# Two sets of sixteen staged tiles, each tile 32 bytes longer, in a two-layer trunk

## The chip, the cores and the metric

The kernel runs on one core of a Trainium2 chip. The metric is the device time of one execution in microseconds.

## What is computed

The reference is a trunk of two layers over 256 tokens of width 2048, in float32. Every sub-layer is preceded by an RMS norm and added to the residual `h`:

```
layer 0   z = gelu(h @ w_in[2048, 4096]); u, v = split(z); v = rms_norm(v)
          s = causal 128x128 mixing of v per head; h += (u * s) @ w_out[2048, 2048]
layer 1   u = h @ w_in[2048, 2048]; y = a diagonal state-space scan of u
          ga, gb = split(gelu(y) @ w_glu[2048, 4096]); h += ga * sigmoid(gb)
after each layer
          z = h @ w_up[2048, 11264]; z = causal convolution of width 3 along the tokens
          gate, val = split(z); h += (silu(gate) * val) @ w_down[5632, 2048]
at the end  rms_norm(h)
```

## The kernel before

**Products in three terms.** TensorE multiplies in the type float32r. To keep float32 accuracy each operand is held as two tiles, a high part and a rest. A weight chunk `w` becomes `wh` (cast on ScalarE, line 124) and `wl` (`w - wh` on VectorE, line 125). The activations, transposed so that the feature dimension is on the partitions, are held the same way: one tile of 128 partitions x 512 columns per chunk of 128 features, with the high parts of the 256 tokens in columns 0 to 255 and the rests in columns 256 to 511.

**X and Gt.** There are two such sets of sixteen tiles. `X[0..15]` holds the normed input of a sub-layer (written by `stage_x`). `Gt[0..15]` holds the input of the product that ends a sub-layer (written by `split_to` or, in the state-space layer, by `emit`). In the second product of layer 1 the same memory as `X` (tag `X0` to `X15`) holds half sums under the name `kept`.

**Two forms of product.** In `group_b_steps` (lines 892 to 894) and in `form_b_steps` (lines 986 to 988) the activation slice is the stationary operand, 128 columns (512 bytes a partition) of an `X` or `Gt` tile, and 512 columns of `wh` or `wl` (2,048 bytes) move past it. For each chunk `k` and each half of the tokens there are three matmuls:

```python
                    T.matmul(ps[:, tt, :], xh, wh, start=k == k_first, stop=False)
                    T.matmul(ps[:, tt, :], xh, wl, start=False, stop=False)
                    T.matmul(ps[:, tt, :], xl, wh, start=False, stop=k == ktot - 1)
```

so six matmuls in a row read one staged tile, and the next six read the next tile. In `form_a_steps` (lines 785 and 786) it is the other way round: 128 columns of `wh` or `wl` are stationary and 512, then 256, columns of an `X` tile move. Every matmul has a weight load of its own, which TensorE begins while the matmul ahead of it is still running.

**Order of the work.** Class `Weights` brings the weights in by DMA on the queue of SyncE (three buffers `raw`), splits them in units of 1024 columns (five buffers each of `wh` and `wl`) and stays four units ahead of the products. The products of the up-projections read `X`, those of the down-projections and of `w_out` and `w_glu` read `Gt`. The FFN goes in three parts of 14, 16 and 14 chunks: an up-projection of two chunk pairs at a time, after it `activate` for each chunk (four transposes into `zt`, the convolution, Silu into a tile `s`, the product with the second half in place, then `split_to(Gt[k], s)`), and then four groups of the down-projection. The scheduler of the tile framework orders each engine's instructions by their dependences.

**Where the tiles lie.** Tiles of the pool `const` are laid out in the order in which they are first asked for, each at a multiple of 32 bytes. After `hn` come `Gt[0..15]` of 2,048 bytes each, then `rbc` (1,024), `rho` (512), `nss` (64), `rtok`, `tv` and `tt_` (8 bytes in 32 each), then `X[0..15]` of 2,048 bytes each, and behind the pool the weight buffers, all of them multiples of 512 bytes long. Modulo 512 every `X` tile therefore begins at the same offset as every weight buffer, and every `Gt` tile at an offset 160 bytes below that (1,024 + 512 + 64 + 96 = 1,696 = 3 x 512 + 160). All slices that a matmul reads lie at multiples of 512 bytes inside their tile or buffer.

Of the kernel before, what the change touches and what calls it, by code (L numbers as in the profile page):

```python
# [9 lines left out]
F32 = mybir.dt.float32  # L10
F32R = mybir.dt.float32r
# [6 lines left out]
P = 128  # L18
D = 2048
NT = 256  # L20
KC = D // P
# [647 lines left out]
def tile_hybrid_trunk(  # L669
# [10 lines left out]
    const = ctx.enter_context(tc.tile_pool(name="const", bufs=1))  # L680
# [54 lines left out]
    conv = const.tile([P, 4, 2 * HC], F32, name="conv")  # L735
    hn = const.tile([P, 2, D], F32, name="hn")
    X = [None] * KC
    Gt = [const.tile([P, 2 * NT], F32R, name=f"Gt{k}") for k in range(KC)]
    rbc = const.tile([P, NT], F32, name="rbc")
    rho = const.tile([P, NH], F32, name="rho")  # L740
    nss = const.tile([P, 2, 8], F32, name="nss")
    rtok = const.tile([P, 2], F32, name="rtok")
    tv = const.tile([P, 2], F32, name="tv")
    tt_ = const.tile([P, 2], F32, name="tt_")

    scr = []
    for name, n in (
# [54 lines left out]

    def stage_x(k, g_col, src):

        xk = X[k] = const.tile([P, 2 * NT], F32R, name=f"X{k}", tag=f"X{k}", bufs=1)
        A.mul(xk[:, :NT], src, g_col[:, k : k + 1])
        V.scalar_tensor_tensor(
            xk[:, NT:], src, g_col[:, k : k + 1], xk[:, :NT].bitcast(F32), ALU.mult, ALU.subtract
        )
# [97 lines left out]
    def ffn(l, g_next, fin=None):  # L907
        cw = conv

        def activate(z, c, q, k):  # L910

            pt = misc_ps.tile([P, 512], F32, name="zt", tag="misc")
            for v in range(2):
                for tt in range(2):
                    T.transpose(  # L915
                        pt[:, v * NT + tt * P : v * NT + (tt + 1) * P],
                        z[:, tt, v * NT + q * P : v * NT + (q + 1) * P], ident,
                    )
            a = fpool.tile([P, 2, NT], F32, name="a", tag="a", bufs=2)
            for v in range(2):  # L920
                cv = c + v * HC
                zt = pt[:, v * NT : (v + 1) * NT]
                A.activation(a[:, v], zt, AF.Identity, bias=cw[:, 3, cv : cv + 1], scale=cw[:, 2, cv : cv + 1])  # L923
                V.scalar_tensor_tensor(  # L924
                    a[:, v, 1:], zt[:, : NT - 1], cw[:, 1, cv : cv + 1], a[:, v, 1:], ALU.mult, ALU.add
                )
                V.scalar_tensor_tensor(  # L927
                    a[:, v, 2:], zt[:, : NT - 2], cw[:, 0, cv : cv + 1], a[:, v, 2:], ALU.mult, ALU.add
                )
            s = fpool.tile([P, NT], F32, name="s", tag="s", bufs=2)  # L930
            A.activation(s, a[:, 0], AF.Silu)
            V.tensor_tensor(s, s, a[:, 1], op=ALU.mult)
            split_to(Gt[k], s)

        for pi, (c0, n, ups, downs) in enumerate(ffn_groups(l)):
            last = pi == len(FFN_PARTS) - 1
            for i in range(n // 2):

                def evac(ps, i=i):
                    z = fpool.tile([P, 2, 512], F32, name="z", tag="z", bufs=2)  # L940
                    for tt in range(2):
                        A.mul(z[:, tt], ps[:, tt], rtok[:, tt : tt + 1])  # L942
                    for q in range(2):
                        pending.append(lambda q=q: activate(z, c0 + 2 * i + q, q, 2 * i + q))

                group_b(X, [4] * 4, evac, {k: (lambda k=k: bg(BG_UP[k])) for k in range(4)})
            nks = [4] * (n // 4) + ([n % 4] if n % 4 else [])
            bgs = {i: (lambda: bg(BG_DOWN)) for i in range(len(nks) - 1)}
            for g in range(4):
                if fin is None or not last:  # L950
                    group_b(Gt, nks, lambda ps, g=g: residual(fpool, g, ps, g_next if last else None), bgs)
                elif g < 3:
                    group_b(Gt, nks, lambda ps, g=g: fin(g, [ps[:, tt, :] for tt in range(2)], (0, 1)))
                else:
                    pss = [acc_ps.tile([P, 2, 512], F32, name="accb", tag="acc")[:, 0, :] for tt in range(2)]
                    form_b(Gt, nks, pss, 10, lambda: fin(g, pss, (0,)))
                    fin(g, pss, (1,))
# [202 lines left out]
    with tc.tile_pool(name="s5", bufs=1) as sp:  # L1160

        Ys = [None] * KC

        def emit(s, yt):
            g, yv = Gt[s], yt.rearrange("p (j k) -> p k j", j=4)
            hi, lo = (g[:, i * NT : (i + 1) * NT].rearrange("p (k j) -> p k j", j=4) for i in range(2))
            A.copy(hi, yv)
            V.tensor_tensor(lo, yv, hi.bitcast(F32), op=ALU.subtract)
            Ys[s] = g

        s5 = S5Tokens(tc, sp, misc_ps, scr, rho, emit)
        rbv = rbc.rearrange("p (k j) -> p j k", j=4)
        sched = {}

        def at(slot, fn, *a):
            sched.setdefault(slot, []).append((fn, a))

        for s in range(KC):
            n = N_OF[s]
            at(n - 1, s5.load, s)  # L1180
            at(n - 1, s5.load1, s)
            at(n, s5.drive, s)
            at(n + 1, s5.take, s)
            at(n + 1, s5.scan, s)
            at(n + 1, s5.load2, s)
            at(n + 2, s5.turn, s)
            at(n + 3, s5.outputs, s)
            at(n + 4, s5.gelu, s)
            at(n + LAT[0], s5.fetch, s)
            at(n + LAT[1], s5.finish, s)  # L1190
        order = (
            s5.gelu, s5.take, s5.finish, s5.fetch, s5.turn, s5.scan, s5.outputs, s5.drive, s5.load2, s5.load, s5.load1
        )

        n_slot = [0]

        def step():
            for fn, a in sorted(sched.pop(n_slot[0], []), key=lambda e: order.index(e[0])):
                fn(*a)
            n_slot[0] += 1  # L1200

        for gi in range(8):

            def evac(p, ps, gi=gi):
                t = sp.tile([P, 2, NT], F32, name="t", tag="t", bufs=tmp[0][1])
                A.copy(t, ps[:, :, NT:])
                z = sp.tile([P, 2, NT], F32, name="z", tag="z", bufs=2)
                V.tensor_tensor(z, ps[:, :, :NT], t, op=ALU.add)
                for i in range(2):
                    s = 2 * gi + i  # L1210
                    u = s5.new_u(s)
                    V.tensor_tensor(u, z[:, i].rearrange("p (k j) -> p j k", j=4), rbv, op=ALU.mult)
                    s5.send(s)

            after = {i: step for i in range(2)}
            if gi == 0:
                after[0] = lambda: (drain(2), make_rbc(sp), step())
            form_a(X, [8, 8], [0, 128], evac, after)

        kept = {}  # L1220

        def glu_keep(i):


            def evac(ps):
                kept[i] = [const.tile([P, 512], F32, name=f"kept{i + a}", tag=f"X{i + a}", bufs=1) for a in range(2)]
                for a in range(2):
                    A.copy(kept[i][a], ps[:, a, :])

            return evac  # L1230

        def glu_evac(i):
            def evac(ps):
                for a in range(2):
                    z = sp.tile([P, 512], F32, name="z", tag="z", bufs=2)
                    V.tensor_tensor(z, ps[:, a, :], kept[i][a], op=ALU.add)
                    A.activation(z[:, NT:], z[:, NT:], AF.Sigmoid)
                    V.tensor_tensor(z[:, :NT], z[:, :NT], z[:, NT:], op=ALU.mult)
                    hv = hn[:, a, i * P : (i + 2) * P]
                    V.tensor_tensor(hv, hv, z[:, :NT], op=ALU.add)  # L1240
                    square_sum(sp, hv, nss[:, a, i // 2 : i // 2 + 1])
                pending.append(lambda: stage_pair(i // 2, cols[:, 3]))
                if i == KC - 2:
                    total_r(nss, 8, rtok)

            return evac

        fa = group_b_steps(Ys, [4, 4], glu_keep(0))
        fb = group_b_steps(Ys, [4, 4], glu_keep(2))
        for f in (fa, fb, fa, fb):  # L1250
            next(f)
            step()
        for f in (fa, fb):
            for _ in f:
                pass
        for i in range(4, KC, 2):
            group_b(Ys, [4, 4], glu_keep(i), {0: step, 1: step})
        assert not sched
        craw = fetch_conv(sp, 1)
        for i in range(0, KC, 2):  # L1260
            group_b(Ys, [4, 4], glu_evac(i), {1: (lambda: place_conv(craw))} if i == 0 else None, 8)
# [69 lines left out]
```

## Time and profile before

| | |
|---|---|
| time, median of 3 runs | 2145.45 us (2145.39 to 2145.92) |
| the profiled execution: its own time | 2145.46 us |
| the profiled execution: span from first to last instruction | 2143.8 us |
| TensorE (PE) busy | 2115.5 us, 99% of the span |
| mean granted TensorE clock | 0.994 |
| VectorE (DVE), ScalarE (ACT), GpSimd (POOL) busy | 1439.3, 1134.9, 90.5 us |
| DMA | 438.59 MB, mean 205 GB/s |

The span is 1.7 us shorter than the time of the execution that it belongs to. Matmuls are pipelined: the end of one is modelled, so the durations of neighbours overlap, and what a matmul costs a chain of matmuls is the step from its start to the start of the next.

### The profile page before, as it was taken

The page shows a single profiled execution, that of the slowest core. Times are in us where ns is not written, and L with a number is a line of the kernel's source. Part 1 is how long each engine was busy: PE and PEld are TensorE (multiplying, and loading weights), DVE is VectorE, ACT ScalarE, POOL GpSimd, SP SyncE. Part 2 cuts the span into 40 slices and gives each one's busy share as a digit, 9 for nine tenths or more (in the row PEclk, how much of TensorE's full clock was granted, in tenths as well). Part 3 has the DMA queues.
Part 4 walks back from the last instruction along what each step waited for, and adds up shares of the span by engine and source line. Part 5 has one row for each costly group of instructions (what it writes and reads, how often), then busy time and mean ns, then how long its engine had stood idle before and what let it go on. Part 6 is the DMA issues. An engine that isn't in the chain of part 4 may idle for free.

```text
span 2143.8 us, 27328 instructions
## 1 busy us (share of the span) xinstructions
PE 2115.5 (99%) x10279; PEld 1740.3 (81%) x10279; DVE 1439.3 (67%) x2123; ACT 1134.9 (53%) x1656; POOL 90.5 (4%) x142
## 2 busy tenths in 40 slices
PE   9999999999999999999998999999999999999998
PEld 7888888888888778888887788888888888888886
DVE  5476677886896645888678766766655656546564
ACT  6544456554555534555456655555544555345553
POOL 1010000000111110000000000000000000000000
PEclk9999999999999999999999999999999999999999
DMA  8655556666777666565799986565556555555553
GB/s 277 199 180 183 188 177 199 222 218 229 215 240 232 217 207 192 189 218 198 231 254 262 271 260 196 177 207 186 176 183 198 189 186 187 181 193 181 192 177 118
DMA packets 358597, 438.59 MB, mean 205 GB/s; under 512 B 31712, under 2 KB 275520, under 8 KB 357824
## 3 DMA queue, kind: packets, MB, share of 16 engines
q1 hardware_dynamic: 349008, 407.94, 60.2%
q0 software_dynamic: 9424, 28.88, 4.6%
q8 instruction: 81, 1.33, 0.3%
q14 instruction: 52, 0.43, 0.1%
q10 hardware_dynamic: 32, 0.01, 0.0%
HBM read 414.66 MB, written 22.02 MB: 204 GB/s over the span
## 4 chain that ended last, share of the span: by engine, by line
PE 95%; DMA 3%; DVE 1%; ACT 1%; issue 0%; SPq 0%; ACTq 0%; DVEq 0%; POOLq 0%
PE accb L892 26%; PE accb L893 26%; PE accb L894 26%; PE acc L785 4%; PE acc L786 2%; PE zt L915 2%; PE accv L986 1%; PE accv L987 1%; PE accv L988 1%; DMA tab<-rd 1%; PE pt L820 1%; PE ps_x L584 1%; DMA w<-in_b_w_glu_dram 0%; DMA ud<-u 0%; ACT wh L124 0%
## 5 line engine op out<-in xcount | busy, mean ns | idle before, releaser
L125 DVE TENSOR_TENSOR wl<-w,wh 128x1024 fp32r<-128x1024 f32 (+1 forms) x721 | 879.3, 1222 | 601.9 <-ACT wh L124 597.8
L124 ACT CAST wh<-w 128x1024 fp32r<-128x1024 f32 (+1 forms) x721 | 754.4, 1050 | 769.4 <-PE accb L894 636.8
L894 PE MATMUL accb<-wh,X 128*128 128x512 f32 x1408 | 552.3, 392 | 0.0
L892 PE MATMUL accb<-wh,X 128*128 128x512 f32 x1408 | 551.7, 392 | 0.0
L893 PE MATMUL accb<-wl,X 128*128 128x512 f32 x1408 | 549.2, 390 | 0.0
L892 PE MATMUL accb<-wh,Gt 128*128 128x512 f32 x1060 | 423.2, 399 | 0.0
L894 PE MATMUL accb<-wh,Gt 128*128 128x512 f32 x1060 | 421.7, 398 | 0.0
L893 PE MATMUL accb<-wl,Gt 128*128 128x512 f32 x1060 | 421.6, 398 | 0.0
L894 PEld LDWEIGHTS accb<-wh,X 128*128 128x128 f32 x1408 | 264.3, 188 | 56.8
L893 PEld LDWEIGHTS accb<-wl,X 128*128 128x128 f32 x1408 | 264.4, 188 | 54.6
L892 PEld LDWEIGHTS accb<-wh,X 128*128 128x128 f32 x1408 | 264.4, 188 | 54.0
L894 PEld LDWEIGHTS accb<-wh,Gt 128*128 128x128 f32 x1060 | 200.3, 189 | 48.4 <-issue 0.2
L892 PEld LDWEIGHTS accb<-wh,Gt 128*128 128x128 f32 x1060 | 200.1, 189 | 48.1
L893 PEld LDWEIGHTS accb<-wl,Gt 128*128 128x128 f32 x1060 | 200.3, 189 | 47.8 <-issue 0.2
L785 PE MATMUL acc<-X,wh 128*128 128x512 f32 x512 | 185.2, 403 | 0.0
L786 PE MATMUL acc<-X,wl 128*128 128x256 f32 x512 | 145.2, 284 | 0.0
L785 PEld LDWEIGHTS acc<-X,wh 128*128 128x128 f32 x512 | 97.7, 191 | 22.0
L923 ACT ACTIVATE a<-zt,conv 128x256 f32<-128x256 f32 x176 | 94.5, 558 | 14.5 <-PE zt L915 8.2
L786 PEld LDWEIGHTS acc<-X,wl 128*128 128x128 f32 x512 | 98.3, 192 | 0.2
L942 ACT ACTIVATE z<-accb,rtok 128x512 f32<-128x512 f32 x88 | 55.8, 685 | 65.8 <-PE accb L894 65.7
L924 DVE SCALAR_TENSOR_TENSOR a<-zt,conv,a 128x255 f32<-128x255 f32 x176 | 77.6, 476 | 13.3 <-ACT a L923 13.3
L927 DVE SCALAR_TENSOR_TENSOR a<-zt,conv,a 128x254 f32<-128x254 f32 x176 | 77.1, 474 | 0.7
(299 smaller groups left out, 1407.1 us busy)
## 6 DMA issues: line engine op xcount, KB each, us to landing
w<-in_f_w_up_dram SPq DMA_DIRECT2D x352, 512.0 KB, 4.6
w<-in_f_w_down_dram SPq DMA_DIRECT2D x80, 1024.0 KB, 5.2
w<-in_b_w_glu_dram SPq DMA_DIRECT2D x64, 512.0 KB, 5.2
w<-in_a_w_in_dram SPq DMA_DIRECT2D x28, 1024.0 KB, 5.3
w<-in_a_w_out_dram SPq DMA_DIRECT2D x16, 1024.0 KB, 5.1
w<-in_b_w_in_dram SPq DMA_DIRECT2D x16, 1024.0 KB, 8.5
w<-in_f_w_down_dram SPq DMA_DIRECT2D x16, 512.0 KB, 3.7
tab<-rd SPq DMA_DIRECT2D x32, 256.0 KB, 6.9
```

What stands on the lines that cost most here:

```text
L124: self.nc.scalar.copy(hi[:, a:b], raw[:, o + a : o + b])
L125: self.nc.vector.tensor_tensor(lo[:, a:b], raw[:, o + a : o + b], hi[:, a:b].bitcast(F32), op=ALU.subtract)
L785: T.matmul(ps, wh, Xt[k], start=k == k_first, stop=False, skip_group_check=True)
L786: T.matmul(ps[:, NT:], wl, Xt[k][:, :NT], start=False, stop=k == ktot - 1, skip_group_check=True)
L892: T.matmul(ps[:, tt, :], xh, wh, start=k == k_first, stop=False)
L893: T.matmul(ps[:, tt, :], xh, wl, start=False, stop=False)
L894: T.matmul(ps[:, tt, :], xl, wh, start=False, stop=k == ktot - 1)
L915: T.transpose(pt[:, v * NT + tt * P : v * NT + (tt + 1) * P], z[:, tt, v * NT + q * P : v * NT + (q + 1) * P], ident,)
L923: A.activation(a[:, v], zt, AF.Identity, bias=cw[:, 3, cv : cv + 1], scale=cw[:, 2, cv : cv + 1])
L924: V.scalar_tensor_tensor(a[:, v, 1:], zt[:, : NT - 1], cw[:, 1, cv : cv + 1], a[:, v, 1:], ALU.mult, ALU.add)
L927: V.scalar_tensor_tensor(a[:, v, 2:], zt[:, : NT - 2], cw[:, 0, cv : cv + 1], a[:, v, 2:], ALU.mult, ALU.add)
L942: A.mul(z[:, tt], ps[:, tt], rtok[:, tt : tt + 1])
```

## The change

Every tile of `Gt` and of `X` (and of `kept`, which uses the memory of `X`) gets eight more float32 columns, 32 bytes, that nothing reads or writes; the name stays bound to the first 512 columns. So tile `k` begins 32·`k` bytes further on, modulo 512, than tile 0. A tile `pad` of 224 bytes is added behind `tt_`. The sixteen `Gt` tiles then take 512 bytes more, `X[0]` and the weight buffers stay at one common offset modulo 512, `Gt[0]` stands 384 bytes below that offset (160 + 224) or, the same thing modulo 512, 128 above it. Relative to the weight buffers `X[k]` begins at 32·`k` and `Gt[k]` at 128 + 32·`k`, modulo 512. The sizes add up to 1,248 bytes a partition, and `s` of the FFN goes from two buffers to one (1,024 bytes less in that pool).

```diff
-    Gt = [const.tile([P, 2 * NT], F32R, name=f"Gt{k}") for k in range(KC)]
+    Gt = [const.tile([P, 2 * NT + 8], F32R, name=f"Gt{k}")[:, : 2 * NT] for k in range(KC)]
...
     tt_ = const.tile([P, 2], F32, name="tt_")
+    const.tile([P, 56], F32, name="pad")
...
-        xk = X[k] = const.tile([P, 2 * NT], F32R, name=f"X{k}", tag=f"X{k}", bufs=1)
+        xk = X[k] = const.tile([P, 2 * NT + 8], F32R, name=f"X{k}", tag=f"X{k}", bufs=1)[:, : 2 * NT]
...
-            s = fpool.tile([P, NT], F32, name="s", tag="s", bufs=2)
+            s = fpool.tile([P, NT], F32, name="s", tag="s", bufs=1)
...
-                kept[i] = [const.tile([P, 512], F32, name=f"kept{i + a}", tag=f"X{i + a}", bufs=1) for a in range(2)]
+                kept[i] = [const.tile([P, 520], F32, name=f"kept{i + a}", tag=f"X{i + a}", bufs=1)[:, :512] for a in range(2)]
```

## Rows read from the trace of the kernel before

**Rows 1.** The page: the span, the engines' busy time and instructions.

```profile
span 2143.8 us, 27328 instructions
PE 2115.5 (99%) x10279; PEld 1740.3 (81%) x10279; DVE 1439.3 (67%) x2123; ACT 1134.9 (53%) x1656; POOL 90.5 (4%) x142
```

**Rows 2.** The chain of work that ended last, shares of the span by engine.

```profile
PE 95%; DMA 3%; DVE 1%; ACT 1%; issue 0%; SPq 0%; ACTq 0%; DVEq 0%; POOLq 0%
```

**Rows 3.** Costliest groups: line, operation, shapes, count; busy us, mean ns; idle before.

```profile
L894 PE MATMUL accb<-wh,X 128*128 128x512 f32 x1408 | 552.3, 392 | 0.0
...
L892 PE MATMUL accb<-wh,Gt 128*128 128x512 f32 x1060 | 423.2, 399 | 0.0
...
L785 PE MATMUL acc<-X,wh 128*128 128x512 f32 x512 | 185.2, 403 | 0.0
...
L986 PE MATMUL accv<-wh,X 128*128 128x512 f32 x128 | 51.0, 398 | 0.0
...
L986 PE MATMUL accb<-wh,Gt 128*128 128x512 f32 x28 | 10.9, 396 | 0.0
```

**Rows 4.** Timeline of PE, an up-projection: start us, duration us (55 matmuls in all).

```profile
1699.71 0.39 PE L893 MATMUL accb<-wl,X 128*128 128x512 f32 x1
1699.94 0.39 PE L894 MATMUL accb<-wh,X 128*128 128x512 f32 x1
1700.16 0.39 PE L892 MATMUL accb<-wh,X 128*128 128x512 f32 x1
...
1711.95 0.39 PE L893 MATMUL accb<-wl,X 128*128 128x512 f32 x1
```

**Rows 5.** Timeline of PE, a down-projection (31 matmuls in all).

```profile
744.88 0.39 PE L892 MATMUL accb<-wh,Gt 128*128 128x512 f32 x1
745.12 0.39 PE L893 MATMUL accb<-wl,Gt 128*128 128x512 f32 x1
...
751.91 0.40 PE L893 MATMUL accb<-wl,Gt 128*128 128x512 f32 x1
```

**Rows 6.** Timeline of PE, an up-projection after transposes: nine steps, then four.

```profile
345.50 0.39 PE L892 MATMUL accb<-wh,X 128*128 128x512 f32 x1
...
347.59 0.39 PE L892 MATMUL accb<-wh,X 128*128 128x512 f32 x1
...
348.49 0.39 PE L893 MATMUL accb<-wl,X 128*128 128x512 f32 x1
```

**Rows 7.** Timeline of PE, products of the first form: five pairs, then three pairs.

```profile
159.25 0.39 PE L785 MATMUL acc<-X,wh 128*128 128x512 f32 x1
...
160.98 0.39 PE L785 MATMUL acc<-X,wh 128*128 128x512 f32 x1
...
170.41 0.39 PE L785 MATMUL acc<-X,wh 128*128 128x512 f32 x1
...
171.47 0.40 PE L785 MATMUL acc<-X,wh 128*128 128x512 f32 x1
```

**Rows 8.** Stretches of 4 and 5: busy us (count) by engine, PEclk, DMA share, GB/s.

```profile
1700.00:1712.00 12.00, 12.00 (x55) 9.94 (x54) 9.61 (x17) 6.65 (x11) 0.00 (x0) 1.00 0.57 185
744.00:752.00 8.00, 8.00 (x44) 6.41 (x35) 4.13 (x5) 3.57 (x7) 2.08 (x2) 1.00 0.68 197
```

**Rows 9.** Timelines of ACT and DVE around two Silus.

```profile
566.40 0.41 ACT L931 ACTIVATE s<-a 128x256 f32<-128x256 f32 x1
...
567.15 0.41 ACT L931 ACTIVATE s<-a 128x256 f32<-128x256 f32 x1
...
571.80 0.43 DVE L801 TENSOR_TENSOR Gt<-s,Gt 128x256 fp32r<-128x256 f32 x1
```

**Rows 10.** Who waited for whom: us in total, times, longest us.

```profile
ACT wh L124 <- PE accb L894: 636.8, 453, 3.7
...
PE ps_x L584 <- DVE wl L125: 2.8, 1, 2.8
```

**Rows 11.** The stretch of the state-space layer, columns as in Rows 8.

```profile
1080.00:1260.00 180.00, 165.85 (x1116) 138.74 (x1115) 144.89 (x186) 111.50 (x164) 8.42 (x15) 0.95 1.01 269
```

## The prediction

> **What bounds the kernel now.** I read the engines' busy time first: TensorE is busy for 2115.5 of 2143.8 us [rows 1], and the chain of work that ended last is 95% TensorE [rows 2]. So nothing but the pace of its matmuls is worth much, and an edit that touches only SBUF addresses can act through that pace alone. The costliest groups give the counts: three lines of 1408 and three of 128 with an `X` tile as stationary operand, 4608 matmuls in all; three of 1060 and three of 28 with a `Gt` tile, 3264; and 512 pairs of the first form, in which `X` moves [rows 3]. The first two kinds are the same instruction, 128x128 against 512 columns, and yet the mean modelled duration is 392 ns with `X` and 399 with `Gt` [rows 3]. The ends are modelled, so I went to the timeline for the steps from start to start. In a clean stretch of an up-projection 54 steps take 12.24 us, 226.7 ns each [rows 4]; in a down-projection 30 steps take 7.03 us, 234.3 ns each [rows 5]. [...] The other engines don't explain the 7.6 ns: in the faster stretch VectorE is busy for 80% and ScalarE for 55% (9.61 and 6.65 of 12 us), in the slower one for 52% and 45% (4.13 and 3.57 of 8 us) [rows 8]. What differs by the layout is where the stationary tile begins against the weight buffer: at the same offset modulo 512 for `X`, 160 bytes below it for `Gt`.
>
> A third reading decides my forecast. Just after transposes the matmuls on `X` don't run at 226.7 ns: nine steps take 2.09 us, and only then do four take 0.90 us [rows 6]. Four steps at 226.7 would be 0.907, so the start between the two runs is shown some 0.007 us late; the nine then take 2.083 us, 231.5 ns each. The fast pace of `X` is thus one into which the chain of matmuls settles, over some nine steps in which address and form stay alike. The first form has two paces as well: five pairs in 1.73 us, 346 ns, and three pairs in 1.06 us, 353 ns [rows 7].
>
> **The change part by part.** *The staggered tiles.* After the change the stationary tile stands at sixteen offsets against the weight buffer, and the offset changes after every six matmuls, when the product goes on to the next tile. The chain had to stay alike for nine steps to settle; now it stays alike for six. I therefore take the unsettled pace, 231.5 ns, for both kinds.
> - `X`: 231.5 - 226.7 = 4.8 ns x 4608 = 22.1 us. Part of it is paid already: `activate` runs once for each of the 88 FFN chunks, and if half of these interrupt products on `X`, 44 x 9 x 4.8 ns = 1.9 us. Left: +20.2 us.
> - `Gt`: 231.5 - 234.3 = -2.8 ns x 3264 = -9.1 us.
> - First form: moving tile and stationary weights part in the same way; 0 to 512 x 7 ns = 3.6 us, and since both paces occur now I take +2 us.
>
> No row shows a residue other than the two, so both ends stay open. From below, the shortest step that the rows show, rounding included, is 0.22 us (the second to the third matmul on `X`, as 0.23 and 0.22 alternate to give 226.7) [rows 4]: at 220 ns everywhere, -6.7 x 4608 - 14.3 x 3264 = -77.6 us. From above, 0.24 us [rows 5]: 13.3 x 4608 + 5.7 x 3264 = +79.9 us. My value lies between the two settled paces and is the only one that a chain of changing state shows.
>
> [...]
>
> *The common shift of `X[0]` and the weight buffers* (1,248 bytes in all at the buffers) moves both operands of the `X` products alike. I cost it at nothing: matmuls on half-tiles and on second buffer halves, multiples of 512 bytes apart, mix in the stretch of 54 even steps [rows 4]. DMA writes the same bytes to other offsets; in the product stretches the DMA share is 0.57 and 0.68 [rows 8], so landings have cover. Only the state-space stretch has none: DMA 1.01 there, TensorE busy for 165.85 of 180 us [rows 11]. If a fifth of its 14 us went or came, that is 3 us either way; I take 0.
>
> *VectorE, ScalarE on the moved tiles*: same instructions, and ScalarE alone waits 636.8 us for TensorE to free weight buffers [rows 10]. Nothing.
>
> *One buffer `s`.* Before, two Silus run 0.75 us apart and the first `s` is read last at 571.80 + 0.43 = 572.23 us [rows 9]. With one buffer the second Silu comes up to 572.23 - 567.15 = 5.1 us later. If it stood in ScalarE's queue in place, the next casts of weights would stand behind it, then the subtraction on VectorE, then TensorE. What hides it: the split runs four units ahead, and a unit is 12 matmuls, 12 x 0.23 = 2.7 us, so 11 us; TensorE waits for `wl` once in the whole execution, for 2.8 us [rows 10]. The tile `Gt[k]` it feeds is wanted a group later. I take 0; with the cover gone in one place, 5 us.
>
> Sum: 20.2 - 9.1 + 2 = +13.1 us on the profiled execution's own 2145.46 us, which is the median of the runs, 2145.45, within 0.01: **2158.6 us**.
>
> **The rivals.**
> *Slower, as summed* (0.50). For it: the settling [rows 6], and that equal offsets are the faster of the two cases that the trace has, so that fifteen of sixteen `X` tiles leave the better case. Against it: two points say little of fourteen others. Its own range: at a step of 230 ns, 3.3 x 4608 - 4.3 x 3264 = +1.2 us and 2147; at the pace of `Gt` everywhere, 7.6 x 4608 = +35 us and 2181.
> *Faster: most offsets are better than both* (0.34). If the stationary and the moving reads disturb each other where they meet, and most of the sixteen offsets keep them apart, `Gt` falls to the pace of `X` and `X` keeps it: -7.6 x 3264 = -24.8 us, 2120.7; if steps reach 0.22 us, 2068. It decides once the mean step over the sixteen offsets is below 229.3 ns, since today's weighted mean is (226.7 x 4608 + 234.3 x 3264) / 7872 = 229.9 and 0.2% of the time is 0.55 ns a step. For it: a difference of 7.6 ns from the offset alone shows that something is to be had. Against it: the case that should be worst by that reasoning, equal offsets, is the better one.
> *No effect* (0.10): the change doesn't do what it says, because the two paces come from something else in the two kinds of product, and the offsets are all alike to the reads. Then 2145. [...] For it: the trace has no third offset. Against it: same form, same clock, and busier neighbours in the faster stretch.
> *The single `s` holds ScalarE* (0.06): the second Silu stands in place where the split is least ahead. The hold of 5.1 us less the longest spare wait of ScalarE, 3.7 us [rows 10], is 1.4 us an occurrence; at a handful of places 5 to 10 us on top of an unchanged pace, 2150 to 2155. It decides when the split's lead is under 5.1 us.
>
> **How the numbers follow.** A measurement of this kernel tells 0.2%, 4.3 us, from no change. Of the first case some 0.04 falls within that; the second is faster throughout; the third is the same; the fourth is slower. Faster 0.34, same 0.14, slower 0.52. The predicted time is that of the first case. The range must hold signs of both kinds: at its low end I leave out the deeper third of the faster case (0.12), at its upper end what lies at and above the pace of `Gt` everywhere (0.07): 2112 to 2182 us. The likeliest case's own range is 2147 to 2181.
>
> **What would show it.** In the timeline of an up-projection the step should no longer be 226.7 ns but change every six matmuls, with a mean near 231.5; in a down-projection it should fall below 234.3. Both mean modelled durations, 392 and 399, should meet near 396. Two Silus should no longer stand 0.75 us apart, and TensorE's waits for `wl` should stay at a few us. The forecast is wrong if the mean steps of both kinds come out below 229 ns (the reads were kept apart), if they stay at 226.7 and 234.3 (offsets don't matter), or if TensorE shows new waits for `wh` or `wl` (the single `s`).

## The result, and the profile after

The changed kernel takes 2160.99 us, the median of 3 runs (2159.54 to 2161.01), against 2145.45 before: a ratio of 1.007, with a 95% interval of 1.0052 to 1.0088. It is slower by 11 to 19 us. The forecast was 2158.6, range 2112 to 2182.

The page of the changed kernel first: span, engines, the chain, and the costliest groups (line, operation, shapes, count; busy us, mean ns; idle before). They answer to [rows 1 to 3]; the line numbers have grown by one.

```profile
span 2159.3 us, 27322 instructions
...
PE 2132.4 (99%) x10279; PEld 1738.9 (81%) x10279; DVE 1440.9 (67%) x2123; ACT 1134.0 (53%) x1656; POOL 90.3 (4%) x142
...
PE 95%; DMA 3%; SPq 0%; DVE 0%; ACT 0%; issue 0%; ACTq 0%; DVEq 0%; POOLq 0%
...
L893 PE MATMUL accb<-wh,X 128*128 128x512 f32 x1408 | 560.4, 398 | 0.0
L895 PE MATMUL accb<-wh,X 128*128 128x512 f32 x1408 | 559.8, 398 | 0.0
L894 PE MATMUL accb<-wl,X 128*128 128x512 f32 x1408 | 555.5, 394 | 0.0
L893 PE MATMUL accb<-wh,Gt 128*128 128x512 f32 x1060 | 421.6, 398 | 0.0
L894 PE MATMUL accb<-wl,Gt 128*128 128x512 f32 x1060 | 419.5, 396 | 0.0
L895 PE MATMUL accb<-wh,Gt 128*128 128x512 f32 x1060 | 419.2, 397 | 0.0
L786 PE MATMUL acc<-X,wh 128*128 128x512 f32 x512 | 183.6, 400 | 0.0
```

The count of TensorE's instructions is the same, its busy time has grown by 16.9 us, and the span by 15.5. The chain still belongs to TensorE. The two kinds of product, 392 and 399 ns in [rows 3], now have nearly one mean. The starts in the timeline give the step: a long stretch of a down-projection (346 steps from the first row to the second), then of the up-projection behind it (118 steps from the third row to the fourth).

```profile
1828.29 0.40 PE L894 MATMUL accb<-wl,Gt 128*128 128x512 f32 x1
...
1908.79 0.39 PE L895 MATMUL accb<-wh,Gt 128*128 128x512 f32 x1
1909.02 0.40 PE L893 MATMUL accb<-wh,X 128*128 128x512 f32 x1
...
1936.45 0.40 PE L894 MATMUL accb<-wl,X 128*128 128x512 f32 x1
```

80.50 us / 346 = 232.7 ns with `Gt`, against 234.3 [rows 5]; 27.43 us / 118 = 232.5 ns with `X`, against 226.7 [rows 4]. One kind lost what the other only partly gained.

**The whole difference, summed.** For an account without remainder I gave each matmul of TensorE the time from its start to the next start in the trace, gaps included, and summed by kind. "Mean step" is the mean of those under 262 ns, that is without the gaps.

| us in the profiled execution | before | after | difference | forecast |
|---|---|---|---|---|
| `X` stationary (4608) | 1059.0, mean step 227.2 ns | 1083.2, 232.5 ns | +24.2 | +20.2 |
| `Gt` stationary (3264) | 772.6, 234.2 ns | 766.2, 232.5 ns | -6.4 | -9.1 |
| first form (1024) | 189.1 | 186.1 | -3.0 | +2 |
| all else on TensorE (transposes, state space, gaps) | 111.8 | 112.5 | +0.7 | 0 |
| sum | | | +15.5 | +13.1 |

Part of what differs from one execution to the next is TensorE's granted clock, which was 0.50 in short stretches: 25.9 us of the profiled execution before (mean granted clock 0.994) and 15.4 us of the one after (0.996). Among 23 other runs of the kernel before, the shortest (2140.03 us) had a mean clock of 0.997 and the longest (2149.01) one of 0.992. Four of the six stretches before stand in the state-space layer, each during or just behind a step of 2.1 to 3.9 us in which TensorE waited. By the mean steps alone, which leave such stretches and the gaps out, `X` and `Gt` would cost 5.3 ns x 4608 - 1.7 ns x 3264 = +18.9 us, where the account has +17.8.

The two parts costed at nothing can be read too. ScalarE's timeline at the two Silus of [rows 9]:

```profile
572.53 0.41 ACT L932 ACTIVATE s<-a 128x256 f32<-128x256 f32 x1
...
578.05 0.42 ACT L932 ACTIVATE s<-a 128x256 f32<-128x256 f32 x1 [0.41 <-DVE Gt L802]
```

They stand 5.5 us apart, no longer 0.75, and the second was released by the split that reads the first `s`. Behind it nothing is late. These are the four largest of TensorE's waits for others (us in total, times, longest us); `wh` and `wl` are not among them, nor further down the list:

```profile
PE ps_x L584 <- DMA ubd<-ud: 9.8, 4, 5.8
PE pt L821 <- DMA hn<-in_x_dram: 2.4, 1, 2.4
PE ps_x L584 <- DVE sp L625: 1.9, 1, 1.9
PE ps_x L584 <- DMA pw<-pd: 1.5, 1, 1.5
```

And the stretch of the state-space layer, columns as in [rows 11], where the moved buffers had no cover from DMA:

```profile
1080.00:1260.00 180.00, 166.61 (x1134) 140.22 (x1133) 145.82 (x186) 112.22 (x165) 8.39 (x15) 0.97 1.02 277
```

TensorE is busy for 166.61 of 180 us, 165.85 before.

### The profile page after: what moved, and what is told of

Read it like the earlier page. It is cut to its first block, busy times and chain, and to the rows that moved or that the text cites. A ratio compares the mean times of both kernels' runs of the same rounds, so it can differ in the third digit from the quotient of the medians.

```text
span 2159.3 us, 27322 instructions
## 1 busy us (share of the span) xinstructions
PE 2132.4 (99%) x10279; PEld 1738.9 (81%) x10279; DVE 1440.9 (67%) x2123; ACT 1134.0 (53%) x1656; POOL 90.3 (4%) x142
## 4 chain that ended last, share of the span: by engine, by line
PE 95%; DMA 3%; SPq 0%; DVE 0%; ACT 0%; issue 0%; ACTq 0%; DVEq 0%; POOLq 0%
PE accb L893 27%; PE accb L895 27%; PE accb L894 26%; PE acc L786 4%; PE acc L787 2%; PE zt L916 2%; PE accv L987 1%; PE accv L989 1%; PE accv L988 1%; DMA w<-in_b_w_glu_dram 1%; DMA ubd<-ud 1%; PE pt L821 1%; PE ps_x L584 0%; PE ps_s L1108 0%; DMA ud<-u 0%; PE ps_k L458 0%
## 5 line engine op out<-in xcount | busy, mean ns | idle before, releaser
L893 PE MATMUL accb<-wh,X 128*128 128x512 f32 x1408 | 560.4, 398 | 0.0
L895 PE MATMUL accb<-wh,X 128*128 128x512 f32 x1408 | 559.8, 398 | 0.0
L894 PE MATMUL accb<-wl,X 128*128 128x512 f32 x1408 | 555.5, 394 | 0.0
```

## The experiments

**The theories.** The sign and the size came out, but the forecast's reason is one of two readings. *Settling*: the chain is slow because its offset changes every six matmuls and it needs nine to settle; any constant offset would settle at a good pace. *Own pace*: each offset between the stationary tile and the moving buffer has a pace of its own, equal offsets are among the best, and staggering averages over mostly worse ones. A third reading, *bystanders*: `s`, `pad` or the moved buffers cost the time.

### The parts one by one

Four kernels, each the kernel before with one edit. In e1 all `Gt` tiles go to the offset of `X`, with nothing staggered:

```diff
     tt_ = const.tile([P, 2], F32, name="tt_")
+    const.tile([P, 88], F32, name="pad")
```

> The kernel before with one tile of 352 bytes added behind tt_, so that all X and all Gt tiles begin at the offset of the weight buffers modulo 512; no stagger, two buffers s. If the offset of the stationary tile against the weight buffer sets the pace of a matmul, the Gt products fall from 234.3 to the 226.7 ns of the X products: -7.6 ns x 3264 = -24.8 us, near 2121 us. If the two paces belong to the two kinds of product and not to the offset: 2145 us and 234.3 ns as before.

e2 takes the single `s` alone:

```diff
-            s = fpool.tile([P, NT], F32, name="s", tag="s", bufs=2)
+            s = fpool.tile([P, NT], F32, name="s", tag="s", bufs=1)
```

> The kernel before with one buffer s in place of two, and nothing else. If the time of the change is all in the matmul steps: 2145 us, within 4 us. If the second Silu holds ScalarE and the weights come late: 5 us or more longer, with new waits of TensorE for wh or wl.

e3 lengthens `X` and `kept` alone:

```diff
-        xk = X[k] = const.tile([P, 2 * NT], F32R, name=f"X{k}", tag=f"X{k}", bufs=1)
+        xk = X[k] = const.tile([P, 2 * NT + 8], F32R, name=f"X{k}", tag=f"X{k}", bufs=1)[:, : 2 * NT]
...
-                kept[i] = [const.tile([P, 512], F32, name=f"kept{i + a}", tag=f"X{i + a}", bufs=1) for a in range(2)]
+                kept[i] = [const.tile([P, 520], F32, name=f"kept{i + a}", tag=f"X{i + a}", bufs=1)[:, :512] for a in range(2)]
```

> Only the X tiles (and kept) are 32 bytes longer; the Gt tiles all stay 160 bytes below the weight buffers modulo 512. By the offsets: X steps at 232.5 ns as in the changed kernel, Gt steps stay at 234.3, so (232.5 - 227.1) x 4608 = +24.9 us, near 2170 us, more than with the whole change. If the loss of the whole change came from the Gt tiles, the pad or the single s: near 2145 us.

e4 lengthens `Gt` alone:

```diff
-    Gt = [const.tile([P, 2 * NT], F32R, name=f"Gt{k}") for k in range(KC)]
+    Gt = [const.tile([P, 2 * NT + 8], F32R, name=f"Gt{k}")[:, : 2 * NT] for k in range(KC)]
```

> Only the Gt tiles are 32 bytes longer; X and the weight buffers stay at one offset. By the offsets: X steps 227.1 ns as before, Gt steps 232.5 in place of 234.3, so -1.8 x 3264 = -5.9 us, near 2139.5 us. If each staggering costs something by itself (a step at every change of tile): 2145 us or more.

Beside them the kernel before took 2143.93 us (median of 23, 2140.03 to 2149.01).

| kernel | median us | ratio (95% interval) | mean step `X`, `Gt`, ns |
|---|---|---|---|
| e1, `Gt` at the offset of `X` | 2120.44 | 0.9889 (0.9874 to 0.9903) | 227.2, 227.2 |
| e2, single `s` | 2145.12 | 1.000 (0.9989 to 1.0010) | 227.2, 234.2 |
| e3, `X` staggered | 2168.05 | 1.011 (1.0095 to 1.0126) | 232.5, 234.2 |
| e4, `Gt` staggered | 2139.17 | 0.9974 (0.9965 to 0.9983) | 227.2, 232.4 |

The same long stretch of the down-projection, in e1's timeline (346 steps):

```profile
1795.03 0.39 PE L894 MATMUL accb<-wl,Gt 128*128 128x512 f32 x1
...
1873.46 0.39 PE L895 MATMUL accb<-wh,Gt 128*128 128x512 f32 x1
```

78.43 us / 346 = 226.7 ns: at the offset of `X`, `Gt` runs exactly as fast as `X`. The 7.6 ns between the two kinds was the offset and nothing else. In e3's timeline an up-projection (106 steps):

```profile
1915.36 0.40 PE L892 MATMUL accb<-wh,X 128*128 128x512 f32 x1
...
1940.02 0.40 PE L893 MATMUL accb<-wl,X 128*128 128x512 f32 x1
```

24.66 us / 106 = 232.6 ns. Each staggered set changes its own products and leaves the other's step alone: e3 costs 24.1 us, e4 gives 4.8 back, and their sum, +19.4, stands just above the 11 to 19 measured for both together. In e2 the Silus part as they did in the changed kernel:

```profile
567.14 0.41 ACT L931 ACTIVATE s<-a 128x256 f32<-128x256 f32 x1
...
572.65 0.42 ACT L931 ACTIVATE s<-a 128x256 f32<-128x256 f32 x1 [0.52 <-DVE Gt L801]
```

and the time stays within about 0.1% either way. One kernel more closes the third reading: e12 is the changed kernel without its `pad`.

```diff
     tt_ = const.tile([P, 2], F32, name="tt_")
-    const.tile([P, 56], F32, name="pad")
```

> The changed kernel without the tile pad: X at 32k as in the changed kernel, Gt at 352 + 32k instead of 128 + 32k, the same sixteen offsets in another order. If the pad only moves the start of the row of offsets: the time of the changed kernel, 2161 us, within 4. If the absolute place of the weight buffers counts (they lie 224 bytes lower): another time, and steps of X other than 232.5 ns.

One run took 2164.39 us (before beside it 2146.25, median of 7), with mean steps of 232.5 ns (`X`) and 232.4 (`Gt`). The moved weight buffers had been tried in e1, where they lie 352 bytes further on and nothing was lost. The bystanders are out.

### One constant offset at a time

To tell settling from own pace nothing may change along the chain. In e5 to e8 all sixteen tiles of a set stand at one offset. A padding tile ahead of the weight buffers shifts the buffers against `X`; a second one behind `tt_` sets where `Gt` falls. They differ in one size (56, 32, 16 and 64 columns):

```diff
     add_ffn(1)
+    wpool.tile([P, 56], F32, name="wpad")
     ws = Weights(nc, wpool, tiles)
...
     tt_ = const.tile([P, 2], F32, name="tt_")
+    const.tile([P, 16], F32, name="pad")
```

> No stagger: a tile of 64 bytes behind tt_ and one of 224 bytes ahead of the weight buffers put all X tiles at 288 and all Gt tiles at 64 against the weight buffers, modulo 512. If every offset has a pace of its own and the changed kernel shows their mean, the steps are those that its tiles at these offsets show, 233.3 ns for X and 232.9 for Gt: 2145.5 + 6.2 x 4.608 - 1.3 x 3.264 = 2169.8 us. If the chain needs some nine like steps to settle, each kind settles in a pace of its own, even or in a short cycle, that the changed kernel does not show; the offset 0 settled at 226.7 where its tile in the changed kernel shows 231.1.

> As e5_x288_gt64, with 128 bytes ahead of the weight buffers: X at 384, Gt at 160. By the steps of the tiles in the changed kernel: 232.9 and 233.3 ns, 2145.5 + 5.8 x 4.608 - 0.9 x 3.264 = 2169.3 us. By settling: steps of their own, not these.

> As e5_x288_gt64, with 64 bytes ahead of the weight buffers: X at 448, Gt at 224. By the steps of the tiles in the changed kernel: 230.9 and 233.3 ns, 2145.5 + 3.8 x 4.608 - 0.9 x 3.264 = 2160.1 us. By settling: steps of their own, not these; the offsets 192 and 448 show the lowest step in the changed kernel, so they may settle at 226.7 ns or less, then near 2140 us.

> As e5_x288_gt64, with 256 bytes ahead of the weight buffers: X at 256, Gt at 32. In the changed kernel the offsets r and r + 256 show like steps, so if the pattern repeats after 256 bytes, X settles at the 226.7 ns of the offset 0 and Gt steps as X does in e5_x288_gt64: 2145.5 + 0 - 3.264 x (234.2 less that step). If it repeats after 512 bytes alone, X does not step at 226.7 ns.

One run each; the kernel before took 2146.08 us beside them. As that kernel's own runs spread from 2140 to 2149 us, the steps decide here and not the times. The long stretches of e5, `Gt` at 64 (346 steps) and then `X` at 288 (106 steps):

```profile
1819.38 0.39 PE L895 MATMUL accb<-wl,Gt 128*128 128x512 f32 x1
...
1900.11 0.39 PE L896 MATMUL accb<-wh,Gt 128*128 128x512 f32 x1
...
1903.14 0.40 PE L894 MATMUL accb<-wh,X 128*128 128x512 f32 x1
...
1927.87 0.39 PE L895 MATMUL accb<-wl,X 128*128 128x512 f32 x1
```

80.73 / 346 and 24.73 / 106 are both 233.3 ns, though the offset stays alike over hundreds of matmuls. Now `X` at 448 in e7, and then at 256 in e8 (106 steps each):

```profile
1897.97 0.39 PE L894 MATMUL accb<-wh,X 128*128 128x512 f32 x1
...
1922.23 0.39 PE L895 MATMUL accb<-wl,X 128*128 128x512 f32 x1
```

```profile
1895.47 0.39 PE L894 MATMUL accb<-wh,X 128*128 128x512 f32 x1
...
1919.50 0.39 PE L895 MATMUL accb<-wl,X 128*128 128x512 f32 x1
```

228.9 ns, and 226.7: at 256 the step is that at 0. The granted clock is 1.00 in all these stretches (0.996 to 0.997 in the mean of these executions). The step thus repeats after 256 bytes (shown at 0 and 256; in the changed kernel the other pairs lie within 1 ns of each other), and eight classes remain. Here they are with their mean steps in ns, in a kernel where all tiles of a set stand there, and in the changed kernel by the tile's class (each step counted to the tile that is loaded during it, that of the next matmul; the means of `X` and `Gt`, and of an offset and its partner 256 further, as a range where they differ by over 0.1):

| offset modulo 256 | all tiles there | in the changed kernel |
|---|---|---|
| 0 | 227.2 (before, `X`; e8) | 231.0 to 231.4 |
| 32 | 233.3 (e5, e8) | 233.2 |
| 64 | 233.3 (e5) | 233.1 |
| 96 | 234.2 (before, `Gt`) | 232.2 to 232.9 |
| 128 | 232.6 (e6) | 231.9 to 232.9 |
| 160 | 233.3 (e6) | 233.3 |
| 192 | 229.0 (e7) | 230.6 to 230.9 |
| 224 | 233.3 (e7) | 233.3 |

The mean of the middle column is 232.0. Of the 5.3 ns that a step of `X` lost (227.2 to 232.5), 4.8 are there without any change along the chain; 0.5 are left for it. That is a balance: by class the change along the chain costs 0 some 4 ns and 192 some 1.8, and 96 gains some 1.6.

The times are 2153.3 (e5), 2162.56 (e6), 2145.24 (e7) and 2141.36 us (e8). By the steps of the changed kernel 2169.8, 2169.3, 2160.1 and 2142.6 were expected, and only e8 came near. e7 came out 14.9 us lower, and 5 us above the 2140 that settling would give: `X` at 448 steps by 229.0 ns where it stands there throughout, and not by the 230.9 of the changed kernel, which is 8.8 us; the rest is spread over the other kinds. e6 came out 6.7 us lower, of which its 232.6 ns in place of 232.9 are 1.4.

e5 missed by 16.5 us, but not by its steps: by the same account as above they cost +26.5 us with `X` and gave 4.2 with `Gt`. The first form took 5.9 us less than before, and all else on TensorE 8.6 less (103.2 us; in the other kernels 108.2 to 115.1). The 8.6 lie in the state-space layer, where TensorE hardly waited. Here are its wait for that layer's DMA, 0.7 us where the changed kernel has 9.8, and the stretch with the columns of [rows 11], TensorE busy for 174.82 us where before has 165.85:

```profile
PE ps_x L584 <- DMA ubd<-ud: 0.7, 2, 0.4
...
1080.00:1260.00 180.00, 174.82 (x1199) 147.26 (x1199) 156.99 (x200) 121.66 (x179) 8.93 (x16) 0.99 1.00 294
```

Why the transfers came in time in this one run is not shown.

### How much the change along the chain costs

e9 holds an offset for four tiles, 24 matmuls, and so separates the two in one pass: `X` stands at 256, 288, 320 and 352, four tiles each (`kept` likewise), and `Gt` at 0.

```diff
     add_ffn(1)
+    wpool.tile([P, 32], F32, name="wpad")
     ws = Weights(nc, wpool, tiles)
...
+    const.tile([P, 24], F32, name="pad")
...
-        xk = X[k] = const.tile([P, 2 * NT], F32R, name=f"X{k}", tag=f"X{k}", bufs=1)
+        xk = X[k] = const.tile([P, 2 * NT + 8 * (k % 4 == 3)], F32R, name=f"X{k}", tag=f"X{k}", bufs=1)[:, : 2 * NT]
```

> Gt at the offset 0 throughout; X at four offsets, each held by four tiles in a row: 256 (like 0) for tiles 0 to 3, then 288, 320, 352. So 24 matmuls pass at one offset instead of 6. Settled paces of these offsets, from the kernels with one offset: 226.7, 233.3, 233.3, 234.3 ns, mean 231.9. If the short stay at one offset is what costs, the tiles 0 to 3 come down from the 231.1 ns that the offset 0 shows in the changed kernel to about (9 x 231.5 + 15 x 226.7) / 24 = 228.5, and the other three stay near 233 to 234. If the stay has no part, they show 231.1. The time is then 2145.5 + 5 x 4.608 - 7.1 x 3.264 = 2145 us by both, within 3 us.

2147.12 us in one run, beside 2146.25 before. An undisturbed pass over the tiles in its timeline: the first matmul on tile 0, then on tiles 1, 4, 8, 12 and 15.

```profile
1624.88 0.39 PE L894 MATMUL accb<-wh,X 128*128 128x512 f32 x1
...
1626.24 0.39 PE L894 MATMUL accb<-wh,X 128*128 128x512 f32 x1
...
1630.33 0.39 PE L894 MATMUL accb<-wh,X 128*128 128x512 f32 x1
...
1635.92 0.40 PE L894 MATMUL accb<-wh,X 128*128 128x512 f32 x1
...
1641.52 0.39 PE L894 MATMUL accb<-wh,X 128*128 128x512 f32 x1
...
1645.73 0.40 PE L894 MATMUL accb<-wh,X 128*128 128x512 f32 x1
```

The block at 256 takes 5.45 us for 24 steps, 227.1 ns; at 288 5.59, 232.9; at 320 5.60, 233.3; at 352 4.21 for 18, 233.9. Each block takes up the pace of its class. Over all passes the four tiles at 256 have means of 230.7, 228.0, 226.7 and 226.8 ns: settling exists, and it lasts about two tiles, but it only matters for the classes with a pace to lose.

e10 goes the other way, with another offset at nearly every step: a 64-byte tile between the first buffers of `wh` and `wl` puts all `wl` 64 bytes above `wh`, `X` and `Gt`, so that the products alternate between the classes 0 and 192.

```diff
             hi = self.pool.tile([P, 1024], F32R, name=f"wh{u}", tag="hi", bufs=5)
+            if u == 0:
+                self.pool.tile([P, 16], F32, name="wpad")
             lo = self.pool.tile([P, 1024], F32R, name=f"wl{u}", tag="lo", bufs=5)
...
+    const.tile([P, 88], F32, name="pad")
```

> X, Gt and the wh buffers at one offset, the wl buffers 64 bytes above it. The slice that is loaded while a wh moves stands at 0, while a wl moves at 448. If the step is set by the operand that moves and the one that is loaded beside it, and each offset keeps its settled pace, two steps of three take 226.7 and one 229.0, mean 227.5: 2145.5 + 0.8 x 4.608 - 6.4 x 3.264 = 2128 us. If a change of offset at every step keeps the chain from settling, 231 to 232 ns: 2145.5 + 4.4 x 4.608 - 2.7 x 3.264 = 2157 us.

2154.29 us in one run (2146.25 before beside it). An up-projection (106 steps):

```profile
1905.56 0.40 PE L895 MATMUL accb<-wh,X 128*128 128x512 f32 x1
...
1930.15 0.40 PE L896 MATMUL accb<-wl,X 128*128 128x512 f32 x1
```

24.59 us / 106 = 232.0 ns, where the classes 0 and 192 taken two to one would give 227.5. So a chain of changing offsets does lose pace, 4.5 ns here, and between good classes this is the larger effect. In the changed kernel it was not, as only two classes of eight are good. With the `wl` buffers the moving operands too change their offset from one matmul to the next; e10 doesn't tell this from the change against the stationary tile.

e11 asks whether 32 bytes is the grain. `Gt` becomes slices of one long tile and begins 16 bytes past the offset of `X`, which stays as it was:

```diff
-    Gt = [const.tile([P, 2 * NT], F32R, name=f"Gt{k}") for k in range(KC)]
+    Gall = const.tile([P, 2 * NT * KC + 8], F32R, name="Gt")
+    Gt = [Gall[:, 4 + 2 * NT * k : 4 + 2 * NT * (k + 1)] for k in range(KC)]
...
+    const.tile([P, 80], F32, name="pad")
```

> X at 0; the Gt tiles are slices of one long tile that begin 16 bytes above the offset of the weight buffers. If only whole steps of 32 bytes count, Gt steps at 226.7 ns and the time is that of the kernel with Gt at 0, 2120 us. If finer offsets have paces of their own: anything from 226 to 234 ns, 2119 to 2145 us.

2135.09 us (2133.7 to 2136.02), ratio 0.995 (0.9933 to 0.9967). The long down-projection (346 steps):

```profile
1806.19 0.39 PE L895 MATMUL accb<-wl,Gt 128*128 128x512 f32 x1
...
1886.92 0.39 PE L896 MATMUL accb<-wh,Gt 128*128 128x512 f32 x1
```

233.3 ns here, 231.9 over all: 16 bytes are enough to leave the fast pace.

## Why the prediction was right, and where its reason was not

- **The bound and the sign.** All of the difference lies on TensorE, as said, and but for some us of clock and gaps it is the pace of the matmuls: the four kinds of the table add up to the span's 15.5 us, and `X`, with the larger count, lost more than `Gt` gained.
- **`X`, +20.2 us: +24.2.** The price of 231.5 ns was 1.0 ns below the mean step of 232.5. The 1.9 us taken off for settling already paid were there (the mean before is 227.2 and not 226.7, 0.5 ns x 4608 = 2.3 us).
- **`Gt`, -9.1 us: -6.4.** The same 1.0 ns too low.
- **First form, +2 us: -3.0.** The total moved against the forecast, but not by the offsets. Between gaps and at a granted clock of 1.00 a pair takes 353.1 ns before and 354.6 after: 1.5 ns x 512 = +0.8 us, the forecast's sign and under half its size. (In e5 and e7 a pair takes 350.9 and 356.8 ns, so this form follows the offset too.) What outweighs it is the clock and the gaps: 22 matmuls of this form stand in the stretches granted 0.50 before, 7.3 us, and 7 after, 2.4 us; the gaps at 1.00 fell from 10.2 to 8.8 us.
- **`s`, the shift, `pad`, 0.** Right: e2 and e12. The cover of the split held with the second Silu 5.5 us behind the first.
- **The reason.** That the offset changes after every six matmuls while the chain needs some nine to settle was true of the chain in kind (some twelve in e9; e10) and not what set the size: 4.8 of the 5.3 ns were the offsets' own paces. That 231.5 ns came near is in good part luck. It was read just after transposes at offset 0, while the mean of eight classes, which no row of before shows, happens to be 232.0. What the trace did hold was a warning: its two offsets gave two settled paces, so an offset can have one of its own. As the step repeats after 256 bytes, fourteen and not fifteen of the sixteen `X` tiles left the better case.
- **The rival on the faster side** was put at the right place, a mean step of 229.3 ns, and fell there: only the classes 0 and 192 lie below it, and none is below 226.7. The bound of 220 ns was never approached. What there was to gain lay in the opposite edit, e1, equal offsets for both sets: 2120.44 us, the fastest kernel of this study, and the 2120.7 that the rival gave for `Gt` at the pace of `X`.
- **No effect.** This rival took the two paces to belong to the two kinds of product, and the offsets to be all alike to the reads. In these products they are not: with one form, one count of instructions and mean granted clocks of 0.994 and 0.996, where the stationary tile lies is worth 7.6 ns a step (234.3 before, 226.7 in e1).

What in the hardware ties the step to the offset stays open. That the stationary and the moving reads disturb each other where they meet, as the rival on the faster side supposed, is not shown: equal offsets should then be the worst, and they step by 226.7 ns; no run here separates the load from the matmul. Why e5 waited less in the state-space layer stays open too.

## What to carry to other kernels

Where a kernel is bound by TensorE, compare the start-to-start steps of like matmuls that differ only in which tile is stationary: a difference at one clock can be the place of that tile, and an unread padding tile tells. Put the stationary tiles and the moving buffers at one offset modulo 256 bytes, all of them, weights' high and low parts included (226.7 ns a step at 0 and at 256; 232.0 with the low parts 64 bytes off); that was worth 1.1% here, in float32r products with 512 moving columns; no other type was run. Staggering bought only the average over the offsets here, 232.5 ns a step, and is to be tried only where the one in use is worse than that average.

## What the runs showed of the hardware

- In these products the step of a float32r matmul with 512 columns and a weight load of its own follows the relative SBUF offset modulo 256 bytes: settled at 226.7 ns at 0, 228.9 at 192, 233.3 at most others, 234.3 at 96, with a granted clock of 1.00 in the stretches read.
- A shift of 16 bytes, finer than the tiles' own 32, takes it from 226.7 to 233.3 in the longest stretch.
- At one offset there can be two settled paces: of e11's products on `Gt`, cut into pieces of twelve steps (the first twelve behind each gap left out), 36 of 183 run at 227 ns and 147 at 233, which is why their mean is 231.9.
- Alternating between offsets whose own paces are 226.7 and 228.9 gives 232.0 (e10): the step depends on the matmuls ahead and not on its own operands alone.
